# A two-layer decoder step on one core: one more head's sample rows turned in 32x32 blocks, GpSimd scaling them and making their low parts, and one head's second value tile moved in two queues

## The chip, the cores and the metric

The kernel runs on one core of a Trainium2 chip. The metric is the device time of one execution in microseconds (us). Before the change the median of three runs is 875.72 us (875.14 to 876.24). The core has a matrix engine (PE, with a separate weight load PEld) and three elementwise engines: VectorE (DVE), ScalarE (ACT) and GpSimd (POOL). SyncE (SP) issues all the transfers. Each engine works through its own queue in order and waits on semaphores for the others.

## The reference

One inference step of a decoder with two layers, for a prompt of 256 tokens and for 8 samples of 8 tokens, so 320 tokens of width 1024. Layer 0 is a spatial-gating MLP, layer 1 is an mLSTM with 8 heads, and a gated MLP with a short convolution follows each. Everything is float32. The change touches only the mLSTM, which for a head computes, per chunk:

```python
sc = jnp.einsum('bhtd,bhsd->bhts', qc, kc) * w_intra
num = w_inter[..., None] * jnp.einsum('bhtd,bhde->bhte', qc, C) \
    + jnp.einsum('bhts,bhse->bhte', sc, vc)
...
kg = kc * g[..., None]
C_new = decay[..., None, None] * C + jnp.einsum('bhsd,bhse->bhde', kg, vc)
```

Here q and k come from a projection, a convolution over time and a silu, v from a projection alone. The 64 sample tokens have their own state C, which is read and updated per sample.

## The kernel before

**Numbers in two parts.** The matmuls take float32 operands as a high part (rounded to float32r) and a low part (the value minus its high part), with three products for each pair. ACT makes a high part by a copy that rounds, and DVE the low part by a subtraction. Each of the 254 weight blocks is loaded by SP into `raw`, gets its high part `wh` on ACT (L183) and its low part `wl` on DVE (L184), and is used by 24 matmuls of 320 columns. There are four `raw` buffers and three of `wh` and `wl`, so the splits run some blocks ahead of PE.

**The loop over heads.** The loop in `layer_b` is skewed: pass h projects head h (six weight blocks: q, k, two of v, two of the output gate), and in between finishes head h-1. At the end of pass h, `k_nat(h)` and `v_nat(h)` bring k and v into the layout with tokens on the partitions: PE transposes 128 tokens at a time into PSUM (tiles `pk` and `pv`), ACT scales and rounds them into high parts (`kgh`, `kgs` for k, `vh` for v), and DVE makes the low parts (`kgl`, the other rows of `kgs`, `vl`, and rows 64 and up of `vh[:, 2]`). Tiles t = 0 and 1 are the prompt's 256 tokens, t = 2 the 64 sample tokens. The factors are g for k (`colsT`, one value per token) and the norm's factor for v (`self.rc`, one value per token).

**The turned heads.** For the heads in `TURNED`, 2 to 6, the sample rows don't go over PE. `turn(h)` has DVE transpose 32x32 blocks of k and v into `kv` (L905, three instructions), and POOL gathers them by eight copies into `nat` (L909), with k doubled onto partitions 64 to 127 (L910). ACT and DVE then make `kgs` (L1015, L1017) and `vh[:, 2]` (L974, L978) from `nat` as they would from PSUM. For heads 0, 1 and 7 the sample rows take three transposes on PE instead, of 128x128 each: one of k in `k_nat` and two of v in `v_nat`.

**What follows in pass h+1.** PE runs two weight blocks (heads up to 3; four for most later heads), then `inter` and `numer` of head h (tile `num`). `numer` begins with two matmuls on `Ps` and `vh[:, 2]`, and ends with three each on tiles t = 0 and 1 of `vh` and `vl`. `state_prompt` reads `kgh`, `kgl`, `vh` and `vl`; `state_sample` reads `kgz`, which POOL masks out of `kgs` (L1043), with `vh[:, 2]` or its shuffled copy `vb` (L988, L994). Later in the pass, `scores` of head h+1 (tile `psc`) needs that head's q and k, convolved on DVE (L863, in place in `bcv`, three instructions each) and split into high and low parts (`kh`, `khl`, L339).

**What sets the order.** PE's instructions stand in the order in which they are written (`pin`). A scheduler places the others on their queues; `behind(ins, first)` and `in_order(...)` add an edge that puts one instruction behind another without a semaphore of its own. `last_split` and `last_low` are the latest `wh` and `wl`. `hi_parts`, `lo_parts`, `ks_hi`, `ks_lo` and `kg_parts` are a head's instructions on `vh`, on the low parts of v, on `kgs` and on `kgh` and `kgl` in turn; `yh` and `yl` are the split of the previous head's output. The value tiles t = 0 and 1 share a PSUM bank, and the ACT copy of tile 1 waits until DVE has read tile 0.

Of the kernel before, what the change touches and what calls it, by code (L numbers as in the profile page):

```python
# [11 lines left out]
F32 = mybir.dt.float32  # L12
F32R = mybir.dt.float32r
AF = mybir.ActivationFunctionType
ALU = mybir.AluOpType
MULT, ADD, SUB, MAX = ALU.mult, ALU.add, ALU.subtract, ALU.max

P = 128
# [8 lines left out]
NH = 8  # L27
DK = 128
DV = 256
# [1 line left out]
KF = DFF // P  # L31
CW = DV + 2
HV = 160
TURNED = range(2, NH - 1)


V_MIX, V_FFN, V_FIN, V_GN, V_LG, V_LB, V_CB, V_FB, V_FW, V_CW = 0, 16, 32, 40, 56, 72, 88, 104, 148, 280
# [23 lines left out]
class Net:  # L61
# [631 lines left out]
    def layer_b(self):  # L693
        nc, tc, I, O = self.nc, self.tc, self.I, self.O
# [4 lines left out]
        with ExitStack() as ctx:  # L699
# [4 lines left out]
            colsT = lp.tile([P, 3, 96], F32, name="cols")  # L704
# [141 lines left out]
            S = [dict() for _ in range(NH)]  # L846
# [42 lines left out]
            def v_epi(h, j, ps):  # L889
# [6 lines left out]
                S[h].setdefault("vT", []).append(vT)  # L896
                if h in TURNED and j:
                    turn(h)

            def turn(h):  # L900

                s = S[h]
                kv = lp.tile([P, 2, 3, 32], F32, tag="kv", name="kv", bufs=1)
                s["nat"] = lp.tile([P, 3, P], F32, tag="nat", name="nat", bufs=1)
                s["turns"] = [nc.vector.transpose(kv[:, :, i, :], x)  # L905
                              for i, x in enumerate((s["ks2"][:, :64], s["vT"][0][:, TP:T], s["vT"][1][:, TP:T]))]
                for c in range(2):
                    for q in range(0, P, 32):
                        nc.gpsimd.tensor_copy(s["nat"][32 * c:32 * c + 32, :, q:q + 32], kv[q:q + 32, c])  # L909
                nc.gpsimd.tensor_copy(s["nat"][64:, 0, :], s["nat"][:64, 0, :])  # L910

            def rows_in(h):
                mb = hp.tile([P, 392], F32, tag="Mb", name="Mb", bufs=3)
# [46 lines left out]
            def v_nat(h):  # L960
                s = S[h]
                n = 2 if h in TURNED else 3
                pv = [self.psa.tile([P, 512], F32, tag="pa", name="pv") for _ in range(n - 1)]
                dsts = [halves(pv[t // 2][:, (t % 2) * DV:(t % 2 + 1) * DV]) for t in range(n)]
                if n < 3:
                    dsts.append(s["nat"][:, 1:])
                for t in range(n):
                    for e in range(2):
                        self.tr(dsts[t][:, e], s["vT"][e][:, t * P:(t + 1) * P], self.ident)
                for t in range(3):  # L970
                    dst = dsts[t]
                    sc = self.rc[:, t:t + 1]
                    a = slice(0, P if t < n else 64)
                    made = nc.scalar.activation(vh[a, t, :, :P], dst[a], AF.Copy, scale=sc[a])  # L974
                    s.setdefault("hi_parts", []).append(made)

                    r, out = (a, vl[:, t, :, :P]) if t < 2 else (slice(64, P) if t < n else a, vh[64:, t, :, :P])
                    low = nc.vector.scalar_tensor_tensor(out, dst[r], sc[r], vh[r, t, :, :P].bitcast(F32), op0=MULT, op1=SUB)  # L978
                    s.setdefault("lo_parts", []).append(low)
                    if t == 1:  # L980
                        self.v_low = low
                    else:
                        self.v_last = low

                if h == 1:
                    for first in S[0]["yh"]:
                        self.behind(first, made)
                vb_first = nc.scalar.copy(vb[:, :, :P], vh[:, 2, :, :P])  # L988
                if h in TURNED:
                    y, hi, k = S[h - 1]["yh"], s["hi_parts"], s["kg_parts"]  # L990
                    self.in_order(y[0], s["ks_hi"][0], y[1], hi[0], hi[1], s["ks_hi"][1], hi[2], k[0], k[2], vb_first)
                    y, lo = S[h - 1]["yl"], s["lo_parts"]
                    self.in_order(y[0], y[1], s["ks_lo"][0], lo[0], s["ks_lo"][1], lo[2], lo[1], k[1], k[3])
                self.vb_made = nc.scalar.copy(vb[:32, :, :P], vh[32:64, 2, :, :P])  # L994

            def v_first(h):
# [3 lines left out]
            def k_nat(h):  # L1000
                s = S[h]
                ks = s["k"][0]
                pool, tag = (self.psm, "pm") if 0 < h < NH - 1 else (self.psa, "pa")
                pk = pool.tile([P, 512], F32, tag=tag, name="pk")
                for t in range(2 if h in TURNED else 3):
                    self.tr(pk[:, t * P:(t + 1) * P], ks[:, t * P:(t + 1) * P] if t < 2 else s["ks2"], self.ident)
                kgh = hp.tile([P, 2, P], F32R, tag="kgh", name="kgh", bufs=1)
                kgl = hp.tile([P, 2, P], F32R, tag="kgl", name="kgl", bufs=1)
                kgs = hp.tile([P, 2, P], F32R, tag="kgs", name="kgs", bufs=1)
                kgz = hp.tile([P, NB, P], F32R, tag="kgz", name="kgz", bufs=1)  # L1010
                g = colsT[:, 2, 32 + h:33 + h]
                src = s["nat"][:, 0] if h in TURNED else pk[:, 2 * P:3 * P]

                for i, (r, o) in enumerate(((slice(0, 32), slice(32, 64)), (slice(32, 64), slice(0, 32)))):
                    made = nc.scalar.activation(kgs[:, i, :], src, AF.Copy, scale=g)  # L1015
                    s.setdefault("ks_hi", []).append(made)
                    s["ks"] = nc.vector.scalar_tensor_tensor(kgs[o, i, :], src[r], g[r], kgs[r, i, :].bitcast(F32), op0=MULT, op1=SUB)  # L1017
                    s.setdefault("ks_lo", []).append(s["ks"])
                s["kg"] = (kgh, kgl, kgs, kgz)
                if h < NH - 1:  # L1020
                    k_mask(h)

                def prompt():
                    self.kg_parts = []
                    for t in range(2):
                        g = colsT[:, t, 32 + h:33 + h]
                        src = pk[:, t * P:(t + 1) * P]
                        self.kg_parts.append(nc.scalar.activation(kgh[:, t, :], src, AF.Copy, scale=g))
                        self.kg_parts.append(nc.vector.scalar_tensor_tensor(kgl[:, t, :], src, g, kgh[:, t, :].bitcast(F32), op0=MULT, op1=SUB))

                if h < NH - 1:
                    prompt()
                    s["kg_parts"] = self.kg_parts
                return prompt
# [157 lines left out]
            vh = hp.tile([P, 3, 2, HV], F32R, name="vh")  # L1192
            vl = hp.tile([P, 2, 2, HV], F32R, name="vl")
            vb = hp.tile([P, 2, HV], F32R, name="vb")
# [15 lines left out]
            def blk():  # L1210
                return self.block(KD, self.x_rhs)
# [12 lines left out]
            for h in range(NH):  # L1224
# [3 lines left out]
                if h:  # L1228
                    ps = S[h].pop("ps") if h == 1 else blk()
                    if h == 2:  # L1230
                        self.behind(self.last_low, S[1]["Pl"])
                        for low in (*S[0]["yl"], S[1]["ks"]):
                            self.behind(low, self.last_low)
                    qk_epi(h, 0, ps)
                    early(h, 0)
                    ps = blk()
                    if h == 1:
                        self.behind(self.last_split, S[0]["hi"])
                    if h - 1 in TURNED:
                        self.behind(S[h - 1]["kg_parts"][2], self.last_split)  # L1240
                        self.behind(self.last_low, S[h - 1]["kg_parts"][1])
                        self.behind(S[h - 1]["kg_parts"][3], self.last_low)
                    qk_epi(h, 1, ps)
                    if h == 1:
                        ps = blk()
                    inter(h - 1)
                    numer(h - 1)
                    early(h, 1)
                    if h > 1:
                        ps = blk()  # L1250
                    with self.behind_split():
# [16 lines left out]
                if h:  # L1268
                    made = state_sample(h - 1, order[1])
                    if not last:  # L1270
                        with tc.issue_after(made.ins):
                            made = normed(h - 1)
# [28 lines left out]
                if h and not last:  # L1301
                    finish(h - 1)
                    made = state_sample(h - 1, 3)
# [10 lines left out]
            h = NH - 1  # L1314
            begin(0)
            self.prefetch(0, self.used + 2)
            self.behind(self.last_low, self.v_last)
            begin(1)
            inter(h)
            numer(h)  # L1320
            ps = blk()
            self.behind(self.last_low, self.kg_parts[1])

            def between():
# [191 lines left out]
```

## Time and profile before

| | |
|---|---|
| median of three runs | 875.72 us |
| the profiled execution's own time | 875.76 us |
| its span in the trace | 874.0 us (1.76 us lie around it) |
| busy in the span: PE, DVE, ACT, POOL | 867.5, 676.8, 504.1, 160.0 us |
| the eight passes of the mLSTM's loop | from 389 to 640 us of the span |

The times within the span are microseconds from its start. In the timelines a row gives start, duration, engine, line, operation, output and inputs, shape and count, and in brackets how long the engine had been idle and what ended it. Matmuls are pipelined, so consecutive ones overlap in such rows: what one costs is the distance from its start to the next one's. A row of a tile's or line's view gives minimum, median and maximum duration in nanoseconds after the count.

### The profile page before, as it was taken

To read this page: it belongs to the slowest core of one execution; us is meant where nothing else is said; L and a number is where in the kernel's file an instruction comes from. 1 tells how busy PE (TensorE), PEld (TensorE's weight loads), DVE (VectorE), ACT (ScalarE), POOL (GpSimd) and SP (SyncE) were. 2 spreads that over 40 slices of the span, in tenths; PEclk is the share of its full clock that TensorE was granted. 3 is DMA by queue.
4 is the path that set the end of the run, shared out by engine and by line. 5 is a ranking of instruction groups with operands and counts; after the bars stand their busy time and mean duration, and the time that the engine had idled before them with its cause. 6 is when DMAs were issued, how large, how long until landed. Compare 5 with 4: busy or idle time off the path is not lost.

```text
span 874.0 us, 16908 instructions
## 1 busy us (share of the span) xinstructions
PE 867.5 (99%) x6373; PEld 850.7 (97%) x6373; DVE 676.8 (77%) x1289; ACT 504.1 (58%) x907; POOL 160.0 (18%) x342
## 2 busy tenths in 40 slices
PE   9999999999999999999999999999999999999997
PEld 7899999999999999999999999999999999999997
DVE  7766996588878865559999998888998888786443
ACT  7557554455555544447877766665866555554442
POOL 3530000031000000005445643121013000000000
PEclk9999999999999999999999999999999999999999
DMA  8855645545445455554746676665664544455541
GB/s 264 260 169 165 183 148 179 168 154 176 155 160 169 156 167 164 156 184 151 239 156 224 237 254 191 199 224 161 204 214 145 169 170 154 160 163 166 156 152 61
DMA packets 54949, 155.74 MB, mean 178 GB/s; under 512 B 7460, under 2 KB 12716, under 8 KB 54868
## 3 DMA queue, kind: packets, MB, share of 16 engines
q1 hardware_dynamic: 54868, 154.67, 55.7%
q8 instruction: 50, 0.82, 0.4%
q14 instruction: 31, 0.25, 0.1%
HBM read 142.66 MB, written 11.99 MB: 177 GB/s over the span
## 4 chain that ended last, share of the span: by engine, by line
PE 98%; DVE 1%; ACT 0%; DMA 0%; issue 0%; POOL 0%
PE pm L86 85%; PE pv_a L86 6%; PE num L86 2%; PE pmix L86 1%; PE pcs L86 1%; PE psc L86 1%; PE pCp L86 1%; PE phn L89 1%; PE pv L89 0%; DMA xT<-in_xv 0%; DVE C L1149 0%; PE pk L89 0%; DVE y_p L682 0%; PE pg L86 0%; ACT wh L183 0%; DVE ylb L1181 0%
## 5 line engine op out<-in xcount | busy, mean ns | idle before, releaser
L184 DVE TENSOR_TENSOR wl<-raw,wh 128x1024 fp32r<-128x1024 f32 (+4 forms) x254 | 301.4, 1187 | 112.4 <-ACT wh L183 111.7
L183 ACT CAST wh<-raw 128x1024 fp32r<-128x1024 f32 (+4 forms) x254 | 255.6, 1007 | 210.5 <-PE pm L86 140.1
L86 PE MATMUL pm<-xh,wh 128*128 128x320 f32 x1216 | 356.1, 300 | 0.0
L86 PE MATMUL pm<-xl,wh 128*128 128x320 f32 x1216 | 354.5, 299 | 0.0
L86 PE MATMUL pm<-xh,wl 128*128 128x320 f32 x1216 | 308.8, 299 | 0.0
L86 PEld LDWEIGHTS pm<-xh,wh 128*128 128x128 f32 x1216 | 229.9, 189 | 0.6 <-issue 0.5
L86 PEld LDWEIGHTS pm<-xl,wh 128*128 128x128 f32 x1216 | 229.9, 189 | 0.0
L86 PEld LDWEIGHTS pm<-xh,wl 128*128 128x128 f32 x1216 | 212.0, 189 | 0.0
L86 PE MATMUL pm<-yh_f,wh 128*128 128x320 f32 x352 | 105.2, 299 | 0.0
L86 PE MATMUL pm<-yl_f,wh 128*128 128x320 f32 x352 | 105.2, 299 | 0.0
L86 PE MATMUL pm<-yh_f,wl 128*128 128x320 f32 x352 | 105.2, 299 | 0.0
L86 PEld LDWEIGHTS pm<-yh_f,wh 128*128 128x128 f32 x352 | 66.5, 189 | 0.0
L86 PEld LDWEIGHTS pm<-yl_f,wh 128*128 128x128 f32 x352 | 66.5, 189 | 0.0
L86 PEld LDWEIGHTS pm<-yh_f,wl 128*128 128x128 f32 x352 | 66.5, 189 | 0.0
L586 DVE SCALAR_TENSOR_TENSOR fcv<-fpad,vecs,fcv 128x336 f32<-128x336 f32 x88 | 49.3, 566 | 1.4
L588 ACT ACTIVATE fgl<-fcv 128x256 f32<-128x256 f32 x44 | 18.3, 415 | 37.3 <-DVE fcv L586 37.3
L86 PE MATMUL pm<-yh_a,wh 128*128 128x320 f32 x128 | 38.4, 300 | 0.0
L86 PE MATMUL pm<-yl_a,wh 128*128 128x320 f32 x128 | 38.3, 299 | 0.0
L86 PE MATMUL pm<-yh_a,wl 128*128 128x320 f32 x128 | 38.3, 299 | 0.0
L581 POOL COPY fns<-fpad 128x2 f32<-128x2 f32 x44 | 12.5, 283 | 138.0 <-DVE fpad L577 137.6
L328 DVE TENSOR_TENSOR xT<-pm,xT 128x320 f32<-128x320 f32 x39 | 19.0, 488 | 23.9 <-PE pm L86 23.9
L86 PE MATMUL pm<-yhb,wh 128*128 128x320 f32 x128 | 35.9, 304 | 0.0
(281 smaller groups left out, 1309.0 us busy)
## 6 DMA issues: line engine op xcount, KB each, us to landing
raw<-in_f_up SPq DMA_DIRECT2D x88, 512.0 KB, 3.5
raw<-in_b_win SPq DMA_DIRECT2D x48, 512.0 KB, 4.0
raw<-in_f_dn SPq DMA_DIRECT2D x32, 448.0 KB, 3.4
C<-in_C SPq DMA_DIRECT2D x32, 258.0 KB, 5.1
out_Cs<-C SPq DMA_DIRECT2D x32, 258.0 KB, 3.9
raw<-in_a_win SPq DMA_DIRECT2D x16, 512.0 KB, 3.6
raw<-in_a_wo SPq DMA_DIRECT2D x16, 512.0 KB, 4.2
raw<-in_f_dn SPq DMA_DIRECT2D x16, 512.0 KB, 3.5
```

The source lines that it names most:

```text
L86: self.pin(self.nc.tensor.matmul(out, lhsT, rhs, start=start, stop=stop, skip_group_check=skip))
L89: self.pin(self.nc.tensor.transpose(out, in_, ident))
L183: self.last_split = self.hold(nc.scalar.copy(wh[:, :kn, :], raw[:, :kn, :]))
L184: self.last_low = nc.vector.tensor_tensor(wl[:, :kn, :], raw[:, :kn, :], wh[:, :kn, :].bitcast(F32), op=SUB)
L328: self.nc.vector.tensor_tensor(x, ps[:, :T], x, op=ADD)
L581: nc.gpsimd.tensor_copy(nst[:, b, 16:18], pd[:, 256:258])
L586: nc.vector.scalar_tensor_tensor(cv, pd[:, i:i + NC], self.vec(w + i * KF), cv, op0=MULT, op1=ADD)
L588: nc.scalar.activation(gl[:, :TP], cv[:, :TP], AF.Gelu_apprx_tanh)
```

## The change

Four things change, all in the mLSTM.

1. `TURNED` begins at head 1 instead of 2, so head 1's sample rows go through `turn` as well, and three of its transposes leave PE.
2. In every turned head POOL multiplies the gathered rows by their factors in `nat` (three instructions, in place of the copy L910), so ACT only rounds them, and POOL subtracts to get the three low parts (`kgs` twice, `vh[64:, 2]` once) in place of DVE.
3. The order within the turned heads is rewritten, with a list of its own for head 1.
4. In the last head, 7, the high part of the second value tile (t = 1) is put ahead of a weight split on ACT, and its low part ahead of a weight's low part on DVE.

```diff
-TURNED = range(2, NH - 1)
+TURNED = range(1, NH - 1)
...
-                nc.gpsimd.tensor_copy(s["nat"][64:, 0, :], s["nat"][:64, 0, :])
+                k, v = s["nat"][:, 0, :], s["nat"][:64, 1:, :].rearrange("p e f -> p (e f)")
+                g = colsT[:64, 2, 32 + h:33 + h].to_broadcast([64, P])
+                nc.gpsimd.tensor_tensor(k[64:], k[:64], g, op=MULT)
+                nc.gpsimd.tensor_tensor(k[:64], k[:64], g, op=MULT)
+                nc.gpsimd.tensor_tensor(v, v, self.rc[:64, 2:].to_broadcast([64, DV]), op=MULT)
...
-                    made = nc.scalar.activation(vh[a, t, :, :P], dst[a], AF.Copy, scale=sc[a])
+                    if t < n:
+                        made = nc.scalar.activation(vh[a, t, :, :P], dst[a], AF.Copy, scale=sc[a])
+                    else:
+                        made = nc.scalar.copy(vh[a, t, :, :P], dst[a])
...
-                    low = nc.vector.scalar_tensor_tensor(out, dst[r], sc[r], vh[r, t, :, :P].bitcast(F32), op0=MULT, op1=SUB)
+                    if t < n:
+                        low = nc.vector.scalar_tensor_tensor(out, dst[r], sc[r], vh[r, t, :, :P].bitcast(F32), op0=MULT, op1=SUB)
+                    else:
+                        low = nc.gpsimd.tensor_tensor(out, dst[r], vh[r, t, :, :P].bitcast(F32), op=SUB)
...
-                    else:
-                        self.v_last = low
-
-                if h == 1:
-                    for first in S[0]["yh"]:
-                        self.behind(first, made)
-                vb_first = nc.scalar.copy(vb[:, :, :P], vh[:, 2, :, :P])
-                if h in TURNED:
+
+                if h in TURNED:
+                    self.behind(s["ks0"], s["lo_parts"][2])
+                vb_first = nc.scalar.copy(vb[:, :, :P], vh[:, 2, :, :P])
+                if h == 1:
                     y, hi, k = S[h - 1]["yh"], s["hi_parts"], s["kg_parts"]
-                    self.in_order(y[0], s["ks_hi"][0], y[1], hi[0], hi[1], s["ks_hi"][1], hi[2], k[0], k[2], vb_first)
+                    self.in_order(hi[0], hi[1], y[0], y[1], hi[2], s["ks_hi"][0], s["ks_hi"][1], k[0], vb_first, k[2])
                     y, lo = S[h - 1]["yl"], s["lo_parts"]
-                    self.in_order(y[0], y[1], s["ks_lo"][0], lo[0], s["ks_lo"][1], lo[2], lo[1], k[1], k[3])
+                    self.in_order(lo[0], y[0], y[1], lo[1], k[1], k[3])
+                elif h in TURNED:
+                    y, hi, k = S[h - 1]["yh"], s["hi_parts"], s["kg_parts"]
+                    self.in_order(y[0], y[1], hi[0], hi[1], hi[2], s["ks_hi"][0], s["ks_hi"][1], k[0], k[2], vb_first)
+                    y, lo = S[h - 1]["yl"], s["lo_parts"]
+                    self.in_order(y[0], y[1], lo[0], lo[1], k[1], k[3])
...
-                    made = nc.scalar.activation(kgs[:, i, :], src, AF.Copy, scale=g)
+                    if h in TURNED:
+                        made = nc.scalar.copy(kgs[:, i, :], src)
+                    else:
+                        made = nc.scalar.activation(kgs[:, i, :], src, AF.Copy, scale=g)
...
+                    if h in TURNED:
+                        s["ks" + str(i)] = nc.gpsimd.tensor_tensor(kgs[o, i, :], src[r], kgs[r, i, :].bitcast(F32), op=SUB)
+                    else:
+                        s["ks"] = nc.vector.scalar_tensor_tensor(kgs[o, i, :], src[r], g[r], kgs[r, i, :].bitcast(F32), op0=MULT, op1=SUB)
...
-                        for low in (*S[0]["yl"], S[1]["ks"]):
+                        for low in S[0]["yl"]:
...
-                    if h - 1 in TURNED:
+                    if h - 1 in TURNED and h > 2:
...
-            self.behind(self.last_low, self.v_last)
+            self.behind(self.last_low, self.v_low)
...
+            self.behind(self.last_split, S[h]["hi_parts"][1])
             self.behind(self.last_low, self.kg_parts[1])
```

**Head 1 on PE and POOL.** The first piece is PE's queue at the end of pass 1, where `k_nat` and `v_nat` transpose into `pk` and `pv` (`qs` is k of all tokens, `ks_5067` k of the samples, `vTb` is v).

```order
 L89 MATMUL pk<-ident,qs 128x128 x2
-L89 MATMUL pk<-ident,ks_5067 128x128
-L89 MATMUL pv<-ident,vTb 128x128 x6
+L89 MATMUL pv<-ident,vTb 128x128 x4
 L86 MATMUL pm<-xh,wh 128x320
```

Of nine transposes six are left, and the weight block behind them follows directly. On POOL, between the small power for head 0's norm (`sl`) and the copies of the next convolution's state (`bns`), this stood there before:

```order
L1101 TENSOR_TENSOR sl<-t_5135,mhalf 128x3
L935 AFFINE_SELECT w<-w 128x128 x2
L938 AFFINE_SELECT w<-w 64x64
L940 AFFINE_SELECT w<-w 64x64
L1043 TENSOR_TENSOR kgz<-kgs,mk 128x512 x2
L858 COPY bns<-bpad_4546 128x3
```

And this stands there now:

```order
L1118 TENSOR_TENSOR sl<-t_5135,mhalf 128x3
L909 COPY nat<-kv 32x3x32 x8
L912 TENSOR_TENSOR nat<-nat,cols 64x128
L914 TENSOR_TENSOR nat<-nat,rc 64x256
L913 TENSOR_TENSOR nat<-nat,cols 64x128
L939 AFFINE_SELECT w<-w 128x128 x2
L942 AFFINE_SELECT w<-w 64x64
L944 AFFINE_SELECT w<-w 64x64
L988 TENSOR_TENSOR vh<-nat,vh 64x2x128
L1033 TENSOR_TENSOR kgs<-nat,kgs 32x128 x2
L1060 TENSOR_TENSOR kgz<-kgs,mk 128x512 x2
L858 COPY bns<-bpad_4546 128x3
```

Eight copies and three multiplications come in ahead of the four masks of `w`, and three subtractions behind them, ahead of `kgz`.

**Head 1 on ACT.** This is ACT's queue now, from the rounding of `vh` for tiles 0 and 1 to the first step of the next head's q convolution (`bcv`); `yhb` is head 0's output, `wh` a weight block.

```order
L979 ACTIVATE vh<-pv,rc 128x2x128 x2
L1197 ACTIVATE yhb<-y_b,gnh 128x320 x2
L981 CAST vh<-nat 64x2x128
L1028 CAST kgs<-nat 128x128 x2
L1045 ACTIVATE kgh<-pk,cols 128x128
L995 COPY vb<-vh 128x2x128
L183 CAST wh<-raw 128x1024
L1045 ACTIVATE kgh<-pk,cols 128x128
L1006 COPY vb<-vh 32x2x128
L861 ACTIVATE bcv<-bpad_4546,vecs 128x344
```

The copy into `vb` (L995) waits for the low part that POOL writes (L988), and the weight split and the second `kgh` now stand behind it; before, that weight split stood ahead of `vb`.

**The last head on ACT.** Before, between the first rounding of `kgs` and the first `kgh` of head 7, with `vh` in the order of tiles 0 and 2 and then 1:

```order
L1015 ACTIVATE kgs<-pk,cols 128x128
L974 ACTIVATE vh<-pv,rc 128x2x128 x2
L1015 ACTIVATE kgs<-pk,cols 128x128
L183 CAST wh<-raw 128x1024
L974 ACTIVATE vh<-pv,rc 128x2x128
L988 COPY vb<-vh 128x2x128
L1028 ACTIVATE kgh<-pk,cols 128x128
```

The same stretch now:

```order
L1030 ACTIVATE kgs<-pk,cols 128x128
L979 ACTIVATE vh<-pv,rc 128x2x128 x2
L1030 ACTIVATE kgs<-pk,cols 128x128
L979 ACTIVATE vh<-pv,rc 128x2x128
L183 CAST wh<-raw 128x1024
L995 COPY vb<-vh 128x2x128
L1045 ACTIVATE kgh<-pk,cols 128x128
```

The weight split and the rounding of tile 1 have changed places, and on DVE the low part of tile 1 and a weight's low part have done the same.

More of the change, by code (lines that the diff above doesn't have):

```diff
@@ L1014, in k_nat @@
                 for i, (r, o) in enumerate(((slice(0, 32), slice(32, 64)), (slice(32, 64), slice(0, 32)))):
-                    made = nc.scalar.activation(kgs[:, i, :], src, AF.Copy, scale=g)
+                    if h in TURNED:
+                        made = nc.scalar.copy(kgs[:, i, :], src)
+                    else:
+                        made = nc.scalar.activation(kgs[:, i, :], src, AF.Copy, scale=g)
                     s.setdefault("ks_hi", []).append(made)
-                    s["ks"] = nc.vector.scalar_tensor_tensor(kgs[o, i, :], src[r], g[r], kgs[r, i, :].bitcast(F32), op0=MULT, op1=SUB)
-                    s.setdefault("ks_lo", []).append(s["ks"])
+                    if h in TURNED:
+                        s["ks" + str(i)] = nc.gpsimd.tensor_tensor(kgs[o, i, :], src[r], kgs[r, i, :].bitcast(F32), op=SUB)
+                    else:
+                        s["ks"] = nc.vector.scalar_tensor_tensor(kgs[o, i, :], src[r], g[r], kgs[r, i, :].bitcast(F32), op0=MULT, op1=SUB)
                 s["kg"] = (kgh, kgl, kgs, kgz)
```

## The prediction

> **What bounds the kernel now.** The page's busy shares come first, then the chain that ended last.
>
> ```profile
> PE 867.5 (99%) x6373; PEld 850.7 (97%) x6373; DVE 676.8 (77%) x1289; ACT 504.1 (58%) x907; POOL 160.0 (18%) x342
> ...
> PE 98%; DVE 1%; ACT 0%; DMA 0%; issue 0%; POOL 0%
> ```
>
> PE is busy for 867.5 of 874.0 us and makes 98% of the chain. So an edit can win time in two ways only: it takes work off PE, or it takes away a wait of PE. It loses time when PE waits anew. What is taken off DVE, ACT or POOL is worth nothing by itself. The view of waits on PE names every stretch in which PE stood still for another engine (line, what it waited for, us in total, times, longest):
>
> ```profile
> ...
> PE num L86 <- DVE vl L978: 0.3, 1, 0.3
> ...
> ```
>
> Of its three rows this one alone lies in the mLSTM: `num` waits once for a low part of v. The change can therefore gain there, and by the transposes that it takes off PE, and nowhere else.
>
> **Three transposes at head 1.** The chain of waits gives the transposes as pieces (start, length, what, count). The first two rows are head 1, with the sample rows on PE, the third is the 48 matmuls of two weight blocks behind them, and the last two are head 2, which is turned before as after.
>
> ```profile
> 437.63 0.33 PE pk L89 x3
> 437.96 0.66 PE pv L89 x6
> 438.61 6.52 PE pm L86 x48
> ...
> 463.61 0.22 PE pk L89 x2
> 463.83 0.44 PE pv L89 x4
> ```
>
> Head 1 spends 0.33 + 0.66 = 0.99 us, head 2 0.22 + 0.44 = 0.66 us. The change gives head 1 the counts of head 2, so PE's queue is shorter by 0.33 us: **-0.33 us**. PE has no wait in that stretch, so all of it comes off the end, unless something is late at a point that PE now reaches 0.33 us sooner.
>
> **The stall in the last head.** PE's timeline, for the numerators of head 6 (first two rows) and head 7 (the rest):
>
> ```profile
> 600.42 0.49 PE L86 MATMUL num<-vh,Ps 128*128 128x258 f32 x2
> ...
> 601.76 0.30 PE L86 MATMUL pm<-xh,wh 128*128 128x320 f32 x1
> ...
> 618.21 0.49 PE L86 MATMUL num<-vh,Ps 128*128 128x258 f32 x2
> ...
> 619.81 0.38 PE L86 MATMUL num<-vl,Ph 128*128 128x258 f32 x1 [0.33 <-DVE vl L978]
> ...
> 620.14 0.30 PE L86 MATMUL pm<-xh,wh 128*128 128x320 f32 x1
> ```
>
> From the first `num` on `Ps` to the next weight block head 6 takes 601.76 - 600.42 = 1.34 us and head 7 takes 620.14 - 618.21 = 1.93 us, for the same eleven matmuls. The difference is 0.59 us: 0.33 us of idle time, and 0.26 us in which the array drains and fills again. That is what the stall costs. What it waits for stands on ACT and DVE:
>
> ```profile
> 616.61 0.37 ACT L1015 ACTIVATE kgs<-pk,cols 128x128 fp32r<-128x128 f32 x1 [0.31 <-DVE kgs L1017]
> 616.87 1.04 ACT L183 CAST wh<-raw 128x1024 fp32r<-128x1024 f32 x1
> 617.81 0.47 ACT L974 ACTIVATE vh<-pv,rc 128x256 fp32r<-128x256 f32 x1
> ```
>
> ```profile
> 617.64 0.34 DVE L1017 SCALAR_TENSOR_TENSOR kgs<-pk,cols,kgs 32x128 fp32r<-32x128 f32 x1
> 618.02 1.23 DVE L184 TENSOR_TENSOR wl<-raw,wh 128x1024 fp32r<-128x1024 f32 x1
> 619.27 0.48 DVE L978 SCALAR_TENSOR_TENSOR vl<-pv,rc,vh 128x256 fp32r<-128x256 f32 x1
> ```
>
> The change swaps the last two rows of each. ACT then rounds tile 1 from 616.9 to 617.4, before DVE has finished `kgs` at 617.98, and DVE makes its low part from 618.0 to 618.5. PE needs it at 619.81 - 0.33 = 619.48 or, counted without the refill, at about 619.3. It is there 0.8 us sooner, so the stall goes whole: **-0.59 us**. What is late instead is the weight's high part by 0.47 us and its low part by 0.48 us. PE first comes to them in the blocks that follow at 620.14 and later, and a block's matmuls with the low part stand last of its 24: that low part would be there at 618.5 + 1.23 = 619.7, and the sixteen matmuls ahead, at some 0.135 us each (from the 6.52 us of the 48 matmuls behind head 1's transposes), start with the block at 619.5, so 2 us are left, an estimate, which covers both. Without that cover PE would wait up to 0.5 us there.
>
> **What the turned heads add to POOL and take from DVE and ACT.** The tile view of `nat` groups what is removed (count: minimum, median, maximum in ns), the view of `kgz` and of line 392 give POOL's price for two inputs.
>
> ```profile
> L910 POOL COPY nat<-nat x5: 289/1168/1374, 461.9 to 579.6; 64x128 f32<-64x128 f32 x5
> L1017 DVE SCALAR_TENSOR_TENSOR kgs<-nat,cols,kgs x10: 337/340/341, 466.0 to 592.2; 32x128 fp32r<-32x128 f32 x10
> L978 DVE SCALAR_TENSOR_TENSOR vh<-nat,rc,vh x5: 478/1365/1366, 468.8 to 592.6; 64x256 fp32r<-64x256 f32 x5
> ```
>
> ```profile
> L392 POOL TENSOR_TENSOR ws_a<-ws_a,trit x4: 733/794/1713, 34.3 to 37.5; 128x256 f32<-128x256 f32 x4
> ```
>
> DVE loses 2 x 0.34 + 0.48 = 1.16 us a head. POOL gains two multiplications of 128 columns, one of 256, one subtraction of 256 and two of 128. The columns set POOL's time in these rows (256 took 0.73 us undisturbed), so I take 0.73 us for 256 and half of it, 0.37 us, for 128: 2 x 0.73 + 4 x 0.37, less the copy's 0.29, is 2.65 us a head. The other end is the disturbed rows: L910 took 1.17 to 1.37 us where it takes 0.29 us alone, so an instruction can be later by some 0.9 to 1.1 us, and line 392's longest took 1.71 us. POOL has room for either; the question is only who waits for it.
>
> **Who waits, at head 1.** The three 32x32 turns take DVE 457.12 - 456.70 = 0.42 us at head 2:
>
> ```profile
> 456.70 0.24 DVE L905 STREAM_TRANSPOSE kv<-ks 128x64 f32<-128x64 f32 x1
> ...
> 457.12 0.52 DVE L951 SCALAR_TENSOR_TENSOR Pf<-psc,w 128x384 f32<-128x384 f32 x1
> ...
> 457.26 4.55 POOL L909 COPY nat<-kv 32x96 f32<-32x96 f32 x8 [0.67 <-DVE kv L905]
> ```
>
> At head 1 they come ahead of the same `Pf`, then at 434.55:
>
> ```profile
> 434.55 0.55 DVE L951 SCALAR_TENSOR_TENSOR Pf<-psc,w 128x384 f32<-128x384 f32 x1
> ...
> 445.01 1.22 DVE L184 TENSOR_TENSOR wl<-raw,wh 128x1024 fp32r<-128x1024 f32 x1
> ...
> 446.40 0.57 DVE L863 SCALAR_TENSOR_TENSOR bcv<-bpad,vecs,bcv 128x344 f32<-128x344 f32 x1
> ...
> 454.25 0.28 DVE L339 TENSOR_TENSOR khl<-qs,kh 128x128 fp32r<-128x128 f32 x1
> ```
>
> ```profile
> 440.06 0.28 POOL L940 TENSOR_SCALAR_AFFINE_SELECT w<-w 64x64 f32<-64x64 f32 x1
> ```
>
> So the turns end at 435.0, the eight copies at 437.1 to 439.6 (eight of 0.26 us by the shortest of L909, or 4.55 us), the three multiplications at 438.6 to 441.1, and the four masks of `w`, which ended at 440.34 before, by 442.2 at the latest. ACT rounds `vh[:, 2]` in about 0.5 us meanwhile, and POOL's low part of v is there at 441 to 443. Three readers wait for it:
>
> ```profile
> 446.08 0.49 PE L86 MATMUL num<-vh,Ps 128*128 128x258 f32 x2
> ...
> 455.27 0.28 PE L86 MATMUL psc<-qh,khl 128*128 128x256 f32 x1
> ```
>
> ```profile
> 442.77 0.42 ACT L988 CAST vb<-vh 128x256 fp32r<-128x256 f32 x1
> ```
>
> PE's `num` on `Ps` comes at 446.08 - 0.33 = 445.75, some 2.7 us later. ACT's `vb` waits for it, and behind `vb` now queue a weight's high part, the second `kgh` (0.4 us), a small copy (0.4) and the first step of the next head's convolution, `bcv` (0.5; these three are estimates from the rows of such tiles above). With the low part at 443.0, `vb` would end at 443.4, the weight's high part at 444.5, `kgh` at 444.9 and `bcv` at 445.8. DVE goes on with `bcv` behind the second `kgl`, before at 446.40, so this chain has 0.6 us to spare; from there DVE works without a gap to `khl`, which ended at 454.53; the matmul on it comes at 455.27 - 0.33 = 454.94. So **0.41 us of slack** stand there at an unchanged DVE, and more if DVE gains by the 1.16 us that it loses. I count this at nothing; without that cover, each us by which the low part is later than 443.0 + 0.6 + 0.41 = 444.0 is a us of PE.
>
> **Heads 2 to 6** have the same pieces on a PE without waits, with DVE relieved by 1.16 us of 25.6 a head and the convolution behind `vb` in the same way. Heads 4 to 6 have two more blocks before `inter`, so nothing there is near. At head 3 `khl` ended 506.57 - 505.18 = 1.39 us before its matmul, and head 2's pass is alike; a `wl` that moves ahead of it by 1.2 us would still leave 0.2 us.
>
> ```profile
> 504.90 0.28 DVE L339 TENSOR_TENSOR khl<-qs,kh 128x128 fp32r<-128x128 f32 x1
> ```
>
> ```profile
> 506.57 0.28 PE L86 MATMUL psc<-qh,khl 128*128 128x256 f32 x1
> ```
>
> I count nothing here: there is no wait to win, and what could be lost is the first rival's price.
>
> **Sum:** 875.76 - 0.33 - 0.59 = **874.84 us**. The profiled execution was 0.04 us above the median of 875.72, so 874.8 stands for both.
>
> **The rivals.**
>
> *A small new wait at `khl` (heads 1 to 3).* If POOL's three instructions ahead of the low part are disturbed by some 0.9 us each, as L910 was, the low part comes at 443.0 + 2.7 = 445.7 instead of 443.0, and PE waits 445.7 - 444.0 = 1.7 us. With two such collisions the wait is 0.8 us, with one none. That gives 874.9 to 876.5, most likely below 875.7. For it speaks that DVE is full just here; against it, that DVE has 1.16 us less to do.
>
> ```profile
> 438.60:464.30 25.70, 25.70 (x207) 24.94 (x206) 25.51 (x63) 18.81 (x43) 14.38 (x22) 1.00 0.58 181
> ```
>
> DVE (third engine in the row of the windows) is busy for 25.51 of 25.70 us in head 1's pass, so it can't catch up by itself.
>
> *POOL's work holds up DVE (the slower side).* Two rows of head 6 overlap:
>
> ```profile
> 588.56 1.04 POOL L1043 TENSOR_TENSOR kgz<-kgs,mk 128x512 fp32r<-128x512 f32 x1 [7.78 <-DVE kgs L1017]
> ...
> 588.82 1.86 DVE L184 TENSOR_TENSOR wl<-raw,wh 128x1024 fp32r<-128x1024 f32 x1
> ```
>
> The `wl` that began inside `kgz` took 1.86 us against 1.22 us at 445.01, so it lost 0.64 us. If every us that POOL gains at head 1 were lost to DVE there (2.65 + 2.10 for the gathering copies), less the 1.16 us that it loses, plus the turns' 0.42, DVE would be later by 4.75 - 1.16 + 0.42 = 4.0 us, of which 0.41 are covered: 3.6 us of wait, and 874.84 + 3.6 = 878.4 us. It is slower than before from a lag of 0.92 + 0.41 = 1.33 us, that is from a third of the full collision. Against it: at heads 2 to 6 most of POOL's added work replaces DVE's in the same stretch, and DVE does not read two operands from SBUF all the time.
> The Trainium skill ("SBUF — State Buffer", section "Who interferes with whom") states such a rule: a DVE instruction with two SBUF inputs contends with a GpSimd instruction that reads SBUF, and whichever starts first holds the shared ports to its end. By that rule the rows at 588.56 and 588.82 are the collision itself, and the trace agrees: 0.64 us lost, where 0.78 us of `kgz` were left. It would make the sum 878.4 if all of POOL's instructions met such an instruction of DVE, and 874.84 if the waits fell on POOL, which has time.
>
> *The stall at head 7 stays*, because the low part of tile 1 is still behind something (the slack is 0.8 us). Then only the transposes count: 875.76 - 0.33 = 875.4 us.
>
> **How the numbers follow.** No new wait, 874.3 to 875.2: 0.60. A small wait at `khl`: 0.25. DVE held up by POOL: 0.07, of which 0.05 beyond 877.5. The stall stays: 0.05. Faster than I can account for, below 874.0: 0.03. About 0.2%, 1.75 us, is what a measurement of this kernel can tell from no change, so "same" is 874.0 to 877.5: faster 0.03, same 0.92, slower 0.05. The range is 874.2 to 876.4: below it are the unaccounted gains, above it the upper end of the wait at `khl` and the collision. The forecast and the stall that stays both lie in it.
>
> **What would show it.** Head 1's pieces should read 0.22 for `pk` x2 and 0.44 for `pv` x4, the wait of `num` for `vl` should be gone, and head 7 should take 1.34 us from `num` on `Ps` to the next block. No wait of `psc` or `num` should appear at heads 1 to 3. POOL's 256-column instructions should take near 0.73 us; above 1.5 us the first rival is at work. If `wl` takes 1.86 us often and DVE's idle time in head 1's pass goes to zero, it is the second. The prediction is wrong if PE shows waits of over 1 us in the mLSTM, or if the time falls with PE's busy time by more than 0.92 us.

## The result and the profile after

The changed kernel takes 876.96 us (median of 22 runs, 876.72 to 877.56), the kernel before 875.75 us (22 runs, 875.08 to 876.37). The ratio is 1.0014, with a 95% interval of 1.0008 to 1.002: slower by 1.2 us, and inside the 0.2% that the prediction named. The prediction was 874.8 us with a range of 874.2 to 876.4, so it was wrong in the sign and the time lies outside its range.

First the view of waits on PE, of the changed kernel (line, what it waited for, us in total, times, longest):

```profile
PE pw L86 <- PEq L1514: 0.8, 1, 0.8
PE psc L86 <- ACT ks L885: 0.5, 1, 0.5
PE pm L86 <- DVE C L1166: 0.4, 1, 0.4
```

The first row lies outside the mLSTM and stands there before as well. The wait of `num` for `vl` is gone as forecast, and two others stand in its place: a weight block (`pm`) waits for a state update `C`, and the scores (`psc`) wait for k's copies. PE's timeline has the places, and the end of head 7's numerator:

```profile
438.66 0.40 PE L86 MATMUL pm<-xh,wh 128*128 128x320 f32 x1 [0.38 <-DVE C L1166]
...
507.76 0.35 PE L86 MATMUL psc<-qh,kh 128*128 128x256 f32 x1 [0.48 <-ACT ks L885]
...
620.00 0.49 PE L86 MATMUL num<-vh,Ps 128*128 128x258 f32 x2
...
621.33 0.30 PE L86 MATMUL pm<-xh,wh 128*128 128x320 f32 x1
```

Head 7 now takes 621.33 - 620.00 = 1.33 us, as head 6 did. So that gain came; the rest was lost elsewhere. To see where, I set the starts of the same matmuls side by side, before and after, and count each from the first matmul of `pg` at 390 us, since single executions differ by up to 0.8 us in what lies ahead of it. A plus means that PE is later than before. Pass h is the loop's pass that projects head h and finishes head h-1.

```
                                     before   after   shift
block behind head 1's transposes     438.37  438.66   +0.28
psc in pass 3                        480.70  481.16   +0.45
block behind head 3's transposes     489.68  490.42   +0.73
psc in pass 4                        506.35  507.76   +1.40
block behind head 4's transposes     515.33  517.03   +1.69
block behind head 7's num            620.14  621.33   +1.18
```

The first place should have been -0.33 and is +0.28, so 0.61 us were lost there. Pass 2 adds nothing. Pass 3 loses 0.45 us and pass 4 loses 0.96 us; 0.1 us is lost before head 7, where 0.6 us come back. The shifts of 0.1 to 0.3 us don't show as waits of PE: the rows of consecutive matmuls overlap, and of the 0.67 us that `psc` loses in pass 4 the view has 0.48.

DVE in pass 4 shows what happened there. These are its timeline and POOL's in the changed kernel:

```profile
496.41 0.34 DVE L1046 SCALAR_TENSOR_TENSOR kgl<-pk,cols,kgh 128x128 fp32r<-128x128 f32 x1
496.84 1.45 DVE L863 SCALAR_TENSOR_TENSOR bcv<-bpad,vecs,bcv 128x344 f32<-128x344 f32 x1
498.21 2.06 DVE L184 TENSOR_TENSOR wl<-raw,wh 128x1024 fp32r<-128x1024 f32 x1
500.19 0.57 DVE L863 SCALAR_TENSOR_TENSOR bcv<-bpad,vecs,bcv 128x344 f32<-128x344 f32 x1
...
501.01 0.68 DVE L863 SCALAR_TENSOR_TENSOR bcv<-bpad,vecs,bcv 128x344 f32<-128x344 f32 x1
```

```profile
494.14 0.73 POOL L988 TENSOR_TENSOR vh<-nat,vh 64x256 fp32r<-64x256 f32 x1 [3.35 <-ACT vh L981]
494.95 1.85 POOL L1033 TENSOR_TENSOR kgs<-nat,kgs 32x128 fp32r<-32x128 f32 x2
496.88 2.31 POOL L1060 TENSOR_TENSOR kgz<-kgs,mk 128x512 fp32r<-128x512 f32 x2
```

A `bcv` takes 1.45 us where the next one takes 0.57, and `wl` takes 2.06 us where it takes 1.22 undisturbed: 0.88 + 0.84 = 1.72 us are lost, beside the two `kgz`. Pass 3 has the same pair of rows (1.44 and 2.06 us). Before, the two `kgz` of pass 4 stood apart and earlier:

```profile
492.04 1.04 POOL L1043 TENSOR_TENSOR kgz<-kgs,mk 128x512 fp32r<-128x512 f32 x1 [3.37 <-DVE kgs L1017]
...
494.37 1.33 POOL L1043 TENSOR_TENSOR kgz<-kgs,mk 128x512 fp32r<-128x512 f32 x1 [0.32 <-DVE kgs L1017]
```

They now wait for POOL's own low parts, which wait 3.35 us for ACT to round `vh[:, 2]`, and so run back to back where DVE makes convolutions and weights' low parts.

### The profile page after: what moved, and what is told of

Read it like the earlier page. It is cut to its first block, busy times and chain, and to the rows that moved or that the text cites. A ratio compares the mean times of both kernels' runs of the same rounds, so it can differ in the third digit from the quotient of the medians.

```text
span 875.2 us, 16945 instructions
## 1 busy us (share of the span) xinstructions
PE 868.3 (99%) x6370; PEld 850.7 (97%) x6370; DVE 672.3 (77%) x1274; ACT 502.6 (57%) x905; POOL 182.6 (21%) x381
## 4 chain that ended last, share of the span: by engine, by line
PE 93%; DVE 4%; ACT 1%; issue 1%; DMA 0%; POOL 0%; DVEq 0%
PE pm L86 81%; PE pv_a L86 6%; PE num L86 2%; PE pmix L86 1%; DVE bcv L863 1%; DVE wl L184 1%; PE pcs L86 1%; PE psc L86 1%; DVE C L1166 1%; PE pCp L86 0%; PE phn L89 0%; DMA xT<-in_xv 0%; PE pv L89 0%; DVE qs L868 0%; ACT wh L183 0%
```

## The experiments

My theory after the result: the wait at 438.66 comes from the three turns, which put DVE's `C` off; the shifts in passes 3 and 4 come from `kgz` meeting `bcv` and `wl`, together with a `wl` that the new order puts ahead of k's last step. The rivals: DVE is simply full from head 1 on and carries its lag along; or POOL's amount of work slows DVE, whatever the single instruction. The times below are medians of 11 runs. The ratios are against the kernel before, run again beside them (medians of 875.92 us for the first four kernels, 875.73 for the next four, 875.82 for the last two). Their intervals are about 0.1% wide to each side, so differences of a few tenths of a us are read from the shifts in the table at the end of this section.

**Last head alone.** The kernel before, with the two edits at head 7.

```diff
-            self.behind(self.last_low, self.v_last)
+            self.behind(self.last_low, self.v_low)
...
+            self.behind(self.last_split, S[h]["hi_parts"][1])
```

> Before, with the last head's two edits alone. Theory: the 0.59 us of the stall at head 7 go whole and nothing else moves, since no other head is touched: 875.75 - 0.59 = 875.16 us, and the view of waits on PE has no row of num on vl. Rival: the swap only shifts the wait (the weight's parts come late in its place): 875.5 to 875.75.

875.17 us, ratio 0.9992 (0.9983 to 1.0001). The profile agrees with the theory to 0.02 us: no shift up to head 7 and -0.60 us there, which is still -0.60 at the last matmul.

**Turns in DVE's gap.**

```diff
-                    self.behind(x, made)
+                    self.behind(x, S[1]["Pf2"] if h == 0 else made)
...
-                    state_sample(0, order[2])
+                    self.behind(S[1]["Pl"], state_sample(0, order[2]))
```

`Pf2` is the second `Pf`, behind which DVE was idle.

> The change, with head 1's three turns on DVE put behind both Pf (into DVE's idle 1.1 us) and Pl put behind the two state updates C that free a PSUM bank. Theory: the wait of the weight block behind head 1's transposes, 0.62 us against an undelayed queue, comes from the turns ahead of that C; the block then starts near 438.0 instead of 438.66 (at least 0.4 us sooner). If the waits in the next passes stand on their own, the time is 876.96 - 0.62 = 876.3 us. Rival: DVE is the bound from there through the fourth pass, so that PE only waits later for what it gains here: the block starts sooner, but the time stays at 876.8 to 877.0.

876.79 us, ratio 1.0009 (1.0 to 1.0018). The timelines of DVE and PE of this kernel at head 1:

```profile
435.11 0.23 DVE L905 STREAM_TRANSPOSE kv<-ks 128x64 f32<-128x64 f32 x1
...
436.92 0.87 DVE L1166 SCALAR_TENSOR_TENSOR C<-C,dec,pcs 128x258 f32<-128x258 f32 x2
```

```profile
438.00 0.38 PE L86 MATMUL pm<-xh,wh 128*128 128x320 f32 x1
...
480.82 0.35 PE L86 MATMUL psc<-qh,kh 128*128 128x256 f32 x1 [0.33 <-ACT ks L885]
```

`C` ends at 437.79 and the block starts at 438.00, 0.34 us sooner than before, without a wait. So the first wait goes with these two edits; the last two runs of this section tell apart what each of them does. But up to `psc` in pass 3 PE now loses 0.49 us (from -0.34 to +0.15) in place of 0.17, and of the 0.62 us won at the first place 0.3 us are left at the end. Both sides were half right: the first wait can be removed on DVE, and passes 3 and 4 are bound by DVE on their own, so that PE's being sooner is partly lost there.

**khl ahead of the weight's low part.**

```diff
+                    if h in (3, 4):
+                        self.behind(self.last_low, khl)
```

> The change, with one weight's low part put behind khl in the third and fourth pass, where the new order has it ahead of k's last step (it stood behind khl before). Theory: that low part (1.2 us) and the collision of kgz with bcv and wl (1.7 us) together make khl late, and either one alone fits into the margin: the wait of psc at 507.8 (0.67 us) goes, and the smaller one at 481 (0.17 us) too: 876.96 - 0.84 = 876.1 us, with kgz's collision still in the trace. Rival: the collision alone is enough to make psc wait: 876.7 to 877.0.

877.23 us, ratio 1.0015 (1.0006 to 1.0024): no better, and this part of my theory fell. The waits on PE of this kernel:

```profile
...
PE pm L86 <- DVE o_b L1174: 0.8, 2, 0.4
PE pm L86 <- DVE C L1166: 0.4, 1, 0.4
```

`psc` waits no more, but two weight blocks wait for `o_b`, which frees their PSUM bank and now stands behind the delayed `wl`. DVE was late as a whole; its order only decided which of its readers waited.

**POOL's part for head 1 alone.** Heads 2 to 6 scaled by ACT and split by DVE, in the order of before.

```diff
+                if h > 1:
+                    nc.gpsimd.tensor_copy(s["nat"][64:, 0, :], s["nat"][:64, 0, :])
+                    return
...
-                    if t < n:
+                    if t < n or h > 1:
...
-                    if h in TURNED:
+                    if h == 1:
...
```

> The change, with heads 2 to 6 scaled and split on ACT and DVE in the order of before; head 1 and head 7 stay changed. Theory: the shifts of the third and fourth pass (0.45 and 1.05 us) belong to these heads' own new work on POOL and go: 876.96 - 1.5 = 875.5 us, kgz no longer runs as a pair beside bcv and wl, and the wait behind head 1's transposes stays (+0.29 us at that block). Rival: DVE's lag from head 1 is carried on into the next passes: waits of 0.4 us or more stay there, 876.2 us or more.

875.75 us, ratio 0.9999 (0.999 to 1.0008). After the block behind head 1's transposes (+0.26) the shift stays at +0.28 through passes 3 and 4: nothing is carried over from head 1, and all of the 1.4 us belongs to the new work and the new order of heads 2 and 3.

**kgz in eight pieces.**

```diff
-                for i in (0, 4):
+                w = 1 if h in TURNED else 4
+                for i in range(0, NB, w):
```

The slices of `kgz` and `mk` take the width `w` in place of 4.

> The change, with kgz of the turned heads made by eight POOL instructions of 128 columns instead of two of 512; nothing else moves. Theory: DVE's bcv (0.57 us alone, 1.45 in the third and fourth pass) and wl (1.22 alone, 2.06) are held until the kgz instruction that began ahead of them ends, so with pieces of about 0.28 us each loses at most 0.3 us instead of 0.85; DVE gets back about 1 us a pass, the shifts of the third and fourth pass shrink from 0.45 and 1.05 us to 0.5 together: 876.0 us. Rival: it is the amount of POOL's work that slows DVE, not the length of one instruction: bcv and wl are slowed as much in sum, 876.8 to 877.1.

875.55 us, ratio 0.9998 (0.9989 to 1.0007). The order on DVE and on ACT is that of the changed kernel, and the whole loss of passes 3 and 4 is gone (+0.27 us from head 1 to head 6). DVE's timeline, and then POOL's, in pass 4 of this kernel:

```profile
495.91 0.81 DVE L863 SCALAR_TENSOR_TENSOR bcv<-bpad,vecs,bcv 128x344 f32<-128x344 f32 x1
496.64 1.41 DVE L184 TENSOR_TENSOR wl<-raw,wh 128x1024 fp32r<-128x1024 f32 x1
497.98 0.71 DVE L863 SCALAR_TENSOR_TENSOR bcv<-bpad,vecs,bcv 128x344 f32<-128x344 f32 x1
...
498.95 0.73 DVE L863 SCALAR_TENSOR_TENSOR bcv<-bpad,vecs,bcv 128x344 f32<-128x344 f32 x1
```

```profile
495.95 5.06 POOL L1061 TENSOR_TENSOR kgz<-kgs,mk 128x128 fp32r<-128x128 f32 x8
```

DVE loses 0.24 + 0.19 + 0.14 + 0.16 = 0.73 us here, in place of 0.88 + 0.84 + 0.11 = 1.83 in the same four instructions of the changed kernel. POOL's `kgz` takes 5.06 us in place of 2.31, and PE loses nothing by it. (An undisturbed piece takes 0.40 us, not the 0.28 of the expectation.) So it isn't the amount of POOL's work (there is more of it now), but how long one instruction of it keeps DVE from starting. The theory's 876.0 was too careful: about 1 us less brings DVE below what PE needs, and the waits vanish instead of shrinking.

**Sample rows first on ACT.**

```diff
-                    self.in_order(y[0], y[1], hi[0], hi[1], hi[2], s["ks_hi"][0], s["ks_hi"][1], k[0], k[2], vb_first)
+                    self.in_order(y[0], hi[2], s["ks_hi"][0], y[1], hi[0], s["ks_hi"][1], hi[1], k[0], k[2], vb_first)
```

> The change, with ACT in heads 2 to 6 rounding the sample rows (vh of tile 2 and the first kgs) ahead of the value tiles, so that POOL's low parts and kgz come some 2 us sooner, beside DVE's work on PSUM tiles. The scheduler moves other instructions with it. Theory: the collision is the cause; kgz no longer meets bcv, which keeps 0.57 us, the waits of psc and of o_b's bank in the third and fourth pass go: 876.96 - 1.5 = 875.5 us. Rival: ACT and DVE are late for the value tiles instead, or kgz meets other instructions with two inputs: 876.5 us or more.

875.44 us, ratio 0.9998 (0.9989 to 1.0007): as the theory had it. POOL and then DVE in pass 4:

```profile
492.31 1.04 POOL L1060 TENSOR_TENSOR kgz<-kgs,mk 128x512 fp32r<-128x512 f32 x1
493.43 0.45 POOL L1033 TENSOR_TENSOR kgs<-nat,kgs 32x128 fp32r<-32x128 f32 x1
493.95 1.91 POOL L1060 TENSOR_TENSOR kgz<-kgs,mk 128x512 fp32r<-128x512 f32 x1
```

```profile
492.86 0.48 DVE L986 SCALAR_TENSOR_TENSOR vl<-pv,rc,vh 128x256 fp32r<-128x256 f32 x1 [0.54 <-ACT vh L979]
...
493.51 1.45 DVE L184 TENSOR_TENSOR wl<-raw,wh 128x1024 fp32r<-128x1024 f32 x1
494.89 0.34 DVE L1046 SCALAR_TENSOR_TENSOR kgl<-pk,cols,kgh 128x128 fp32r<-128x128 f32 x1
495.15 0.41 DVE L855 TENSOR_TENSOR bpad<-pm,rb 128x256 f32<-128x256 f32 x1
...
495.61 1.33 DVE L184 TENSOR_TENSOR wl<-raw,wh 128x1024 fp32r<-128x1024 f32 x1
```

The first `kgz` is 4.6 us sooner than in the changed kernel. The two now run beside instructions that read one operand from PSUM (`vl` beside the first, `kgl` and `bpad` beside the second): these keep their 0.48, 0.34 and 0.41 us. The first `wl` loses 0.23 us, but to POOL's low part `kgs`, inside which it starts; the second `kgz` starts inside that `wl` and is held up itself (1.91 us), and the second `wl` loses 0.11 us to its end. `bcv` meets no `kgz` any more. The scheduler moved other instructions as well, so this run alone would not prove the cause; with the run before it, it does.

**Head 1 and head 7 only, turns in the gap.** The fourth kernel with the second one's edits.

> Heads 2 to 6 as before, head 1 and head 7 changed, the three turns of head 1 in DVE's gap and Pl behind C. Theory: both gains whole and no wait: 875.75 - 0.33 - 0.59 = 874.8 us, with the block behind head 1's transposes at 438.0 and no wait of PE in the mLSTM. Rival: DVE in the third pass has no room for PE's being sooner, and a wait of 0.3 us or more shows there: 875.1 to 875.5.

875.02 us, ratio 0.999 (0.9981 to 0.9999). The view of waits has no row of the mLSTM any more, and the block behind the transposes is 0.34 us sooner. At the end the profile has -0.72 us, 0.2 us short of the theory. They are lost at one matmul of the block behind head 4's transposes, where the shift goes from -0.34 to -0.12. That block multiplies the outputs of heads 0 to 3, and its sixteenth matmul reads the low part of the second half of head 3's output:

```profile
516.52 0.53 DVE L1202 SCALAR_TENSOR_TENSOR ylb<-y_b,gnh,yhb 128x320 fp32r<-128x320 f32 x1
```

```profile
517.11 0.40 PE L86 MATMUL pm<-ylb,wh 128*128 128x320 f32 x1
```

`ylb` ends at 517.05, and the matmul starts 0.06 us later. In the kernel before `ylb` ended 0.31 us ahead of this matmul. In all six kernels where 0.11 us or less are left, 0.05 to 0.22 us are lost here (the changed kernel's 0.1 us too), and in the six where 0.20 us or more are left nothing is.

**Both mends on the whole change.** The turns in the gap and the sample rows first on ACT.

> The whole change with both mends, the turns in the gap and the sample rows first on ACT. Theory: all three waits gone, 874.9 us, the change's own gain. Rival: at least one of them is only moved: 875.5 to 876.5 us.

874.82 us, ratio 0.9989 (0.998 to 0.9998): the lowest median of all, 0.9 us below the kernel before (by the interval 0.2 to 1.8 us), and within 0.1 us of the theory. The profile gives -0.95 us at head 7.

**Eight pieces with the turns in the gap**, first with `Pl` still ahead of `C`, then behind it.

> kgz in eight pieces, and head 1's three turns in DVE's gap; Pl stays ahead of C. Theory: without the turns ahead, DVE's two C end where they did before, near 438.3 us, so the block behind the transposes starts where it did before (438.37) and the three transposes less still win nothing: 875.55 - 0.29 = 875.3 us. Rival: the turns are the whole of that wait, and the block starts at 438.04: 874.9 us.

> As the run before it, and Pl behind the two C. Theory: C ends by 437.9, the block starts at 438.04, and both gains of the change are whole: 875.55 - 0.62 = 874.9 us with no wait of PE in the mLSTM. Rival: PE sooner by 0.33 us finds DVE late in the third and fourth pass again: 875.2 us or more.

875.36 us (ratio 0.9994, 0.9985 to 1.0003) and 875.23 us (0.9992, 0.9983 to 1.0001). In the profiles the block behind the transposes has a shift of -0.02 us in the first and -0.34 us in the second. So the turns cost 0.3 us of the wait, and the other 0.3 us were never to be had while `C` stood behind `Pl`. The second run's median is 0.3 us above the theory; its profile shows 0.06 us lost up to pass 3 and 0.07 us at the matmul on head 3's `ylb`; the rest is within the median's interval of 0.1%.

The shifts of all kernels, from PE's timelines in the same way as above (us, against before):

```
                             block 438  psc 481  block 490  psc 506  block 515  block 620
the change                      +0.28    +0.45     +0.73     +1.40     +1.69      +1.18
last head alone                 -0.02     0.00      0.00      0.00      0.00      -0.60
turns in gap, Pl behind C       -0.34    +0.15     +0.43     +1.06     +1.35      +0.86
khl before wl                   +0.26    +0.28     +0.90     +0.92     +2.04      +1.53
POOL's part for head 1 alone    +0.26    +0.28     +0.28     +0.28     +0.28      -0.32
kgz in eight                    +0.25    +0.27     +0.27     +0.28     +0.28      -0.33
samples first on ACT            +0.26    +0.28     +0.28     +0.28     +0.28      -0.32
head 1, 7 only, turns in gap    -0.34    -0.34     -0.34     -0.34     -0.34      -0.72
both mends                      -0.35    -0.36     -0.35     -0.35     -0.35      -0.95
eight, turns in gap             -0.02     0.00      0.00      0.00      0.00      -0.55
eight, turns, Pl behind C       -0.34    -0.28     -0.28     -0.27     -0.27      -0.80
```

## Why the prediction was wrong

**The stall at head 7: right.** Forecast -0.59 us, measured -0.60 us with the edits alone and 1.33 us for the numerator. The weight's parts, later by half a us, were not missed.

**The three transposes: right in size, wrong in effect.** The chain's pieces are gone from PE, and 0.33 us can be had (-0.34 with the turns in the gap and `Pl` behind `C`). The step that failed is "all of it comes off the end, unless something is late at a point that PE now reaches 0.33 us sooner". I followed that only to the readers of the low part in pass 2, and not to the very next matmul. Its bank is freed by two `C` on DVE, and these are the rows of before that I should have set against it:

```profile
437.42 0.87 DVE L1149 SCALAR_TENSOR_TENSOR C<-C,dec,pcs 128x258 f32<-128x258 f32 x2
```

```profile
438.37 0.38 PE L86 MATMUL pm<-xh,wh 128*128 128x320 f32 x1
```

`C` ended at 438.29 and the block started at 438.37, 0.08 us later. Where PE does wait, in the changed kernel, it starts 0.06 us behind `C` (438.60 and 438.66), so the slack was 0.02 us (with eight pieces and the turns in the gap, but `C` still behind `Pl`, the block wins just these 0.02 us). That is where I was about to make PE sooner by 0.33 us and, with the turns, DVE later. I counted the turns' 0.42 us only in the second rival and against `khl`, 20 us further on. By way of `Pf`, ACT and `Ps` they reach `C` as well, which ends 0.31 us later. So the term of -0.33 us is one of +0.28: 0.61 us.

**Who waits at head 1's low part: right in the number, in part by luck.** POOL's timeline in the changed kernel, and the views of the two multiplications (minimum, median, maximum in ns):

```profile
442.44 0.80 POOL L988 TENSOR_TENSOR vh<-nat,vh 64x256 fp32r<-64x256 f32 x1 [1.89 <-ACT vh L981]
```

```profile
L914 POOL TENSOR_TENSOR nat<-nat,rc x6: 607/608/1709, 438.5 to 582.5; 64x256 f32<-64x256 f32 x6
```

```profile
L912 POOL TENSOR_TENSOR nat<-nat,cols x6: 395/824/1361, 438.0 to 581.2; 64x128 f32<-64x128 f32 x6
```

The low part of v was there at 443.24, a little behind the forecast 441 to 443 and ahead of the 444.0 from which PE would have lost, and pass 2 shows no shift. But what set this time wasn't POOL's work, which the forecast added up: POOL was done at 440.55 and stood idle for 1.89 us until ACT had rounded `vh[:, 2]`, which the prediction took to be done meanwhile. That number came near for another reason than the one given, and the same wait for ACT, 3.35 us in pass 4, is what moves `kgz` in the next passes. POOL's undisturbed prices were about right: 0.73 us for the subtraction of 256 columns in pass 4, as estimated, 0.61 and 0.40 us for the multiplications against 0.73 and 0.37, and 0.45 us for a subtraction of 128 against 0.37.

**Heads 2 to 6 at nothing: wrong.** This step cost 1.4 us. I had two of its pieces, the margin of 1.39 us at `khl` of pass 4 and the `wl` of 1.2 us that moves ahead of it, and let them cancel to 0.2 us. The third piece, that `kgz` comes later and as a pair, and so beside `bcv` and `wl`, I did not have. The second rival has its mechanism, with a chance of 0.07, but neither its place nor its size: I worked it out for head 1, with all of POOL's added time lost to DVE (3.6 us), where `bcv` in truth lost 0.62 us in pass 2 (0.75 and 1.01 us against 0.57). In passes 3 and 4 it is 1.72 us of DVE each. What `psc` of pass 4 waits for is ACT's copy of k, before and after:

```profile
504.69 0.30 ACT L885 COPY ks<-qs 128x128 f32<-128x128 f32 x1
```

```profile
507.36 0.29 ACT L885 COPY ks<-qs 128x128 f32<-128x128 f32 x1
```

It ends 2.66 us later, where PE comes 0.73 us later and the copy had 506.35 - 504.99 = 1.36 us to spare. Of the 1.93 us by which it falls behind PE, DVE's rows account for 1.72 (the collision) + 1.21 (the `wl` ahead of k's last step) - 1.16 (the work taken off DVE) = 1.77 us. In passes 5 to 7 `wl` is held up too (1.42 and 1.84 us in pass 6), and PE loses nothing by it between 518 and 619 us: for heads 4 to 6 the prediction was right.

The sum by what was measured: 875.75 - 0.33 + 0.61 + 0.45 + 0.96 + 0.1 - 0.6 = 876.94 us, where 876.96 was measured.

**The argument against that rival** was that DVE doesn't read two operands from SBUF all the time. This holds on average, but not where it counts: behind the new low parts `kgz` falls into the stretch where DVE does little else. And the first rival's price was worked out from a late `vb`, which did not happen (it ended at 443.68 us); the wait of `psc` that it named came, in passes 3 and 4 and from another cause.

**The range** was too narrow for the same reason: it took in a small wait at `khl` and no second and third one, and left out the collision.

## What to carry to other kernels

When an edit makes the bottleneck engine reach a point sooner, look at the very next instruction that reuses a buffer there, and set the end of its last reader against the new time; a view of waits does not show that only some hundredths of a us are left. When work moves to another engine, ask not only how long it takes there but when what follows it will now run, and beside which instructions of its neighbour: a shift of some 4 us in `kgz` cost more than the moved work gained. Where a long instruction of one engine holds up another, cutting it into pieces can be better than making it cheaper.

## What the runs showed of the hardware

A DVE instruction with both operands in SBUF was held up for most of the length of the `kgz` beside it: `bcv` took 1.45 us instead of 0.57 and `wl` 2.06 instead of 1.22 beside a `kgz` that takes 1.04 us alone. With `kgz` in pieces of 0.40 us the same two took 0.81 and 1.41. DVE instructions with an operand in PSUM beside it kept their time (`vl` 0.48, `kgl` 0.34, `bpad` 0.41 us). POOL is held up in the same way: a `kgz` took 1.91 us beside a `wl`. The Trainium skill ("SBUF — State Buffer", section "Who interferes with whom") has this as an exclusive lock that is held for the full instruction, and says that a DVE instruction with at most one SBUF input, outside the two-port performance modes, does not contend with GpSimd. The traces agree with both, and the run with eight pieces is a direct test of the first. Which of two instructions that start 0.04 us apart had the lock first (`bcv` at 496.84 and `kgz` at 496.88 us) the rows don't tell. What I had not expected is that more and longer work on POOL (5.06 instead of 2.31 us for `kgz`) can leave DVE with less delay (0.73 instead of 1.83 us).
